# The first FFN's pools of a one-core encoder layer end ahead of its low-rank stage

## The chip, the cores and the metric

The kernel runs on one core of a Trainium2 chip. The core has a matrix engine (TensorE, PE in the profile), three engines for elementwise work (VectorE or DVE, ScalarE or ACT, GpSimd or POOL), SyncE (SP), which issues most transfers, and 16 DMA engines. Tiles lie in on-chip memory with 128 rows (partitions); matrix products land in PSUM, eight banks of 128 × 512 words. What counts is the device time of one launch in microseconds (us).

## The reference, cut to what matters

The kernel computes one layer for 1024 tokens of width 1024, in float32:

```python
x = x + 0.5 * post1(FFN1(pre1(x)))             # SwiGLU, hidden width 2816
z = pre2(x) @ w_in                             # attention q|k|v, then r|k|v, decay-, iclr-, gate-down
# attention group: 8 heads, rotary, three dilated bands
# RWKV-7 group: u = u + mu_prev * (prev - u) + mu_next * (next - u), then
w_logit = w0 + jnp.einsum('bsdr,drc->bsdc', jnp.tanh(wd), w2)      # wd: 2 directions x 64
decay = jnp.exp(-jnp.exp(-jax.nn.softplus(-w_logit) - 0.5))
a = jax.nn.sigmoid(a0 + jnp.einsum('bsdr,drc->bsdc', ad, a2))      # ad: 2 directions x 64
# ... forward and backward delta-rule scans with decay, a, k, v, r; gate with g
x = x + post2(concat(attn, rwkv) @ w_out)
x = x + 0.5 * post3(FFN2(pre3(x)))
```

The two lines with `w2` and `a2` are the low-rank stage: from 64 numbers per token and direction to 512, for the decay and for the in-context rate.

## The kernel before, in words

The layer runs as a chain of stages. FFN1 and FFN2 form their products in blocks with fewer multiplications than the plain product needs. Every large product is done in a split form: both factors are cut into a high and a low part (names that end in h and l), and three products, high × high, low × high, high × low, are added up in PSUM. ACT makes the high part, DVE the low one.

FFN1 ends in `down`, which hands finished token tiles to `hand_over`; this adds the residual, stores h1 and turns the normalised tiles into the operand x2. Half of the tokens at a time, `ready` (in `run`) then projects three column tiles of w_in, 12, 13 and 14: the inputs of decay, rate and gate. Their products are still named gu, with weights gh and gl. `finish_low` brings them out of PSUM (ACT: us and u), forms the token shift on DVE, and for decay and gate a tanh. `low_rank` is called for "w" (decay) and "a" (rate). For each of two directions it builds weights w (tile name rh) and the low part `low` (rl), and two operands rx, each with 64 rows of high parts and 64 of low parts. For four groups of 128 channels and two halves of the tokens it makes two products into one bank (lg): rh by rx over 128 rows, and rl by rx over the 64 rows of the high part:

```python
T.matmul(q, w[:, cs], x[half], start=True, stop=False)
T.matmul(q, low[hs, cs], x[half][hs], start=False, stop=True)
```

That makes 64 lg products. ACT takes a tanh from each pair into ra; for the decay ACT then scales ra, DVE forms a running sum in it (a scan, reset at every chunk by the tile `reset`), and SP stores ra to DRAM as d_w or d_a. The scan stage later loads these back as th_w and th_a.

Next come `project_rwkv` (products zr, 576 of them) and `project_tokens` (zq, 1152), with weights loaded as zraw by SP and split into zh (ACT) and zl (DVE). Then attention is interleaved with the preparation (`prep`: lp and others), solution and chaining of the scan's chunks, followed by the gate and normalisation, `out_project` (products pw), and FFN2.

Nothing of this runs in the order in which it is written. A recorder, `_Tape`, notes all operations; `wire` finds which must follow which, also through the reuse of tiles and banks; `cost` gives each a duration; `sweep` lists them by rank, and the table LEADS adds an amount to the ranks of stretches of recorded operations (from, to, lead). `GATED` names groups of products that are to start only when their inputs are due. `play` (line 486) then issues everything, each engine in its fixed order. So every instruction has the line of `play`, and is told by its tile's names.

Two kinds of pool matter. A pool's memory is handed to later pools when it closes; `ffn1` and `hand1` (tiles gh, gl, junk) and the PSUM pool `ps_1` (tags gu and d, four banks each) close at the end of the `with` block, after `low_rank`; the pool `zr`, opened behind it, lies over the place of the FFN1 pools. The `ring` is the weight ring that lives through the whole kernel (tags raw, wh, wl, tmp).

## Time and profile before

| | us |
|---|---|
| median of 3 runs | 2276.98 (2271.82 to 2277.48) |
| profiled execution | 2268.24 |
| its span in the profile | 2266.4 |
| TensorE busy | 2177.2 (96%) |
| last gu of FFN1's end, start | 712.87 |
| lg products, first and last start | 713.10, 750.8 |
| first zr, start | 754.90 |
| first lp, start | 876.3 |

The profile shows one execution. A row of a timeline has the start, the duration, the engine, the operation with its output and inputs, and in brackets how long the engine stood idle before it and what it then waited for. PE's durations overlap, since products are pipelined; how long a product occupies PE is read from one start to the next. A row of windows gives, for a stretch, the busy time and number of instructions of each engine, then the clock that was granted to TensorE (1.00 is full speed), the busy share of the DMA engines and their rate.

### The profile page before, as it was taken

The page shows a single profiled execution, that of the slowest core. Times are in us where ns is not written, and L with a number is a line of the kernel's source. Part 1 is how long each engine was busy: PE and PEld are TensorE (multiplying, and loading weights), DVE is VectorE, ACT ScalarE, POOL GpSimd, SP SyncE. Part 2 cuts the span into 40 slices and gives each one's busy share as a digit, 9 for nine tenths or more (in the row PEclk, how much of TensorE's full clock was granted, in tenths as well). Part 3 has the DMA queues.
Part 4 walks back from the last instruction along what each step waited for, and adds up shares of the span by engine and source line. Part 5 has one row for each costly group of instructions (what it writes and reads, how often), then busy time and mean ns, then how long its engine had stood idle before and what let it go on. Part 6 is the DMA issues. An engine that isn't in the chain of part 4 may idle for free. (4 is left out here: it accounts for less than half of the span.)

```text
span 2266.4 us, 41176 instructions
## 1 busy us (share of the span) xinstructions
PE 2177.2 (96%) x15236; PEld 1793.6 (79%) x15236; DVE 1499.2 (66%) x2606; ACT 1059.0 (47%) x2031; POOL 708.2 (31%) x1034
## 2 busy tenths in 40 slices
PE   7999999999999999999789998998899999999998
PEld 5888888888876688999768787776688888888886
DVE  8767767775586345772464658647987777777566
ACT  6333333354578445452556666455533333325453
POOL 2244444520000000557275562131024444452000
PEclk9999999999998899999798999999999999999999
DMA  5354444586662537773896675597535544458665
GB/s 148 117 166 166 160 158 148 194 291 193 189 209 81 208 110 199 196 227 111 239 223 166 157 182 136 144 299 261 158 103 175 169 158 158 140 200 296 193 201 183
DMA packets 373054, 408.71 MB, mean 180 GB/s; under 512 B 76659, under 2 KB 279283, under 8 KB 372853
## 3 DMA queue, kind: packets, MB, share of 16 engines
q1 hardware_dynamic: 324096, 303.18, 45.0%
q0 software_dynamic: 30704, 94.44, 11.9%
q10 hardware_dynamic: 18052, 8.46, 1.4%
q8 instruction: 120, 1.97, 0.4%
q14 instruction: 82, 0.66, 0.1%
HBM read 271.69 MB, written 134.28 MB: 179 GB/s over the span
## 5 line engine op out<-in xcount | busy, mean ns | idle before, releaser
L486 ACT ACTIVATE wh<-raw 128x512 fp32r<-128x512 f32 x264 | 162.8, 628 | 378.9 <-PE gu L486 313.4
L486 DVE TENSOR_TENSOR row<-gu,row 128x512 f32<-128x512 f32 x308 | 204.3, 686 | 108.0 <-PE gu L486 64.2
L486 DVE TENSOR_TENSOR wl<-raw,wh 128x512 fp32r<-128x512 f32 x264 | 215.2, 824 | 88.2 <-ACT wh L486 55.8
L486 POOL TENSOR_TENSOR row<-row 128x512 f32<-128x512 f32 x88 | 123.7, 1406 | 435.3 <-DVE row L486 424.2
L486 PE MATMUL gu<-xh,wh 128*128 128x512 f32 x704 | 250.1, 394 | 0.6 <-DVE row L486 0.6
L486 PE MATMUL gu<-xl,wh 128*128 128x512 f32 x704 | 249.0, 392 | 0.2 <-DVE xl L486 0.2
L486 PE MATMUL gu<-xh,wl 128*128 128x512 f32 x704 | 248.9, 391 | 0.0
L486 DVE TENSOR_TENSOR gwl<-graw,gwh 128x512 fp32r<-128x512 f32 (+1 forms) x176 | 112.0, 642 | 111.7 <-PE pd L486 80.4
L486 PE MATMUL pd<-gh,gwl 128*128 128x512 f32 x616 | 181.3, 391 | 0.5 <-DVE gwl L486 0.5
L486 PE MATMUL pd<-gh,gwh 128*128 128x512 f32 x616 | 180.7, 391 | 0.0
L486 PE MATMUL pd<-gl,gwh 128*128 128x512 f32 x616 | 180.5, 390 | 0.0
L486 ACT ACTIVATE gwh<-graw 128x512 fp32r<-128x512 f32 (+1 forms) x176 | 100.6, 576 | 140.9 <-PE pd L486 115.8
L486 PEld LDWEIGHTS gu<-xh,wh 128*128 128x128 f32 x704 | 133.2, 190 | 28.1 <-DVE row L486 1.0
L486 PEld LDWEIGHTS gu<-xl,wh 128*128 128x128 f32 x704 | 132.6, 189 | 27.6 <-DVE xl L486 0.5
L486 PEld LDWEIGHTS gu<-xh,wl 128*128 128x128 f32 x704 | 132.2, 188 | 27.4 <-issue 0.2
L486 PEld LDWEIGHTS pd<-gh,gwl 128*128 128x128 f32 x616 | 115.7, 188 | 25.4 <-DVE gwl L486 1.1
L486 PEld LDWEIGHTS pd<-gh,gwh 128*128 128x128 f32 x616 | 115.6, 188 | 24.1
L486 PEld LDWEIGHTS pd<-gl,gwh 128*128 128x128 f32 x616 | 115.7, 188 | 23.9
L486 ACT ACTIVATE gh<-raw 128x512 fp32r<-128x512 f32 x160 | 99.2, 629 | 51.9 <-PE pd L486 31.0
L486 POOL TENSOR_TENSOR ws<-ws 128x512 f32<-128x512 f32 x88 | 119.9, 1362 | 3.0
L486 DVE TENSOR_TENSOR gl<-raw,gh 128x512 fp32r<-128x512 f32 x160 | 114.4, 722 | 9.0 <-ACT gh L486 8.9
L486 POOL DMA_DIRECT2D d_hid<-row x154 | 83.7, 547 | 90.3 <-DVE row L486 76.0
(299 smaller groups left out, 5130.6 us busy)
## 6 DMA issues: line engine op xcount, KB each, us to landing
d_hid<-row POOLq DMA_DIRECT2D x154, 256.0 KB, 2.7
graw<-d_hid SPq DMA_DIRECT2D x132, 256.0 KB, 2.7
raw<-in_ffn_w_gate_dram SPq DMA_DIRECT2D x88, 256.0 KB, 3.2
raw<-in_ffn_w_up_dram SPq DMA_DIRECT2D x88, 256.0 KB, 3.1
ws<-in_ffn_w_down_dram SPq DMA_DIRECT2D x88, 256.0 KB, 3.7
d_ws<-ws POOLq DMA_DIRECT2D x88, 256.0 KB, 2.9
raw<-d_ws SPq DMA_DIRECT2D x88, 256.0 KB, 3.5
raw<-in_ffn_w_down_dram SPq DMA_DIRECT2D x66, 256.0 KB, 3.7
```

The costliest lines, as they stand in the source:

```text
L486: i = getattr(getattr(self.nc, op.eng), op.method)(*op.args, **op.kwargs).ins
```

## The change

The pools ffn1, hand1 and ps_1 get a stack of their own, s_f1, which closes after `finish_low` and ahead of `low_rank`. `low_rank` takes its tiles rh, rl and rx from the ring's tags wh and wl, and its banks from a new pool ps_l of three. `reset` becomes a 512-wide tile in the ring, and the pools for the next stages (pw, po, zr) open ahead of `low_rank`. The second half's gu products of `ready` use the banks with tag d. The unused half of the rl rows is zeroed by GpSimd, and the second lg product runs over all 128 rows. The scaling of the decay goes from ACT to DVE, in halves of 512, and so does the scan. The three mixing constants are loaded at the start of the kernel. The products of `out_project` are renamed op and enter GATED. The scheduler's costs change for transfers with 64 rows or fewer, for long 64-row products and for DVE's tensor_scalar. LEADS is another table, with 45 entries in place of 27, so that instructions move all over the kernel.

```diff
@@ -35,12 +35,16 @@
 LEADS = (
-    (173, 348, -479), (1428, 1481, 2437), (1440, 1452, 10001), (2180, 2899, 3481), (8375, 8561, 532),
...
+    (173, 304, -13864), (735, 754, -5727), (1432, 1454, -4125), (1676, 1677, -11252), (2515, 2520, -13828),
@@ -98,7 +102,7 @@
     FREE, NEAR = ("ps_w",), 3000
-    GATED = {"s3": 0, "s12": 0, "pt3": 0, "pt12": 0, "lp": 0, "bp": 0, "yq": 0, "gate": 1, "bonus": 1}
+    GATED = {"s3": 0, "s12": 0, "pt3": 0, "pt12": 0, "lp": 0, "bp": 0, "yq": 0, "gate": 1, "bonus": 1, "op": 2}
 
@@ -220,7 +224,7 @@
                         for op in users.get(name, ()):
-                            if op.eng != "tensor":
+                            if op.eng != "tensor" or self.GATED[base] == 2:
                                 given[first].update((g, 1) for g in given[op] if g.eng is None or self.GATED[base] and g.eng != "tensor")
@@ -260,9 +264,10 @@
         if op.method == "dma_start":
-            op.took, op.late = (560 if op.eng == "gpsimd" else 360), 1500
             runs = [math.prod(q[1] for q in a.ap) // (a.ap[-1][1] if a.ap[-1][0] == 1 else 1) for a in (x, *op.ins)]
             size = math.prod(q[1] for q in x.ap) * 4
+            half = any(a.tensor.name in self.home and a.ap[0][1] <= 64 for a in (x, *op.ins))
+            op.took, op.late = (560 if op.eng == "gpsimd" else 360) + 200 * half, 1500 + (600 if half else 0)
             op.moved = (14 * max(runs) + 0.0384 * size) / 16
@@ -272,7 +277,7 @@
             elif w.dtype == F32R:
-                op.took = max(58, 13 + 0.418 * n)
+                op.took = max(58, 13 + 0.418 * n) * (2 if n > 256 and k <= 64 else 1)
             elif m <= 32:
@@ -282,7 +287,7 @@
             rate = 1.04
-            if op.method in ("tensor_copy", "memset") and all(
+            if op.method in ("tensor_copy", "tensor_scalar", "memset") and all(
                     self.home.get(a.tensor.name, (None,))[0].space != PSUM for a in op.ins if a.tensor.name in self.home):
@@ -764,9 +769,9 @@
 
-    def product(self, psum, x, hl, which):
-
-        return self.product_into([psum.tile([128, 512], F32, name="gu", tag="gu") for _ in which], x,
+    def product(self, psum, x, hl, which, tag="gu"):
+
+        return self.product_into([psum.tile([128, 512], F32, name="gu", tag=tag) for _ in which], x,
                                  [(h[:, k, :], l[:, k, :]) for h, l in hl for k in range(4)], which)
@@ -989,20 +994,21 @@
 
-    def low_rank(self, p, ring, rows, psum, nm, y, reset):
+    def low_rank(self, ring, rows, psum, nm, y, reset):
 
...
         raw = self.slab(ring, self.io["rwkv_" + nm + "2"].rearrange("o d r (a b) -> (o d r) a b", a=4)).rearrange("p a b -> p (a b)")
-        low = p.tile([128, 512], F32R, name="rl", tag="gh", bufs=GB)
         bias = self.w0h if nm == "w" else self.a0h
+        tile = lambda name, tag: ring.tile([128, 512], F32R, name=name, tag=tag, bufs=WB)
         for d in range(2):
             hs, os = slice(d * 64, d * 64 + 64), slice(64 - d * 64, 128 - d * 64)
-            w = p.tile([128, 512], F32R, name="rh", tag="gh", bufs=GB)
+            w, low = tile("rh", "wh"), tile("rl", "wl")
             A.activation(w[hs], raw[hs], AF.Copy)
             A.activation(w[os], raw[hs], AF.Copy)
+            self.nc.gpsimd.memset(low[os].bitcast(F32), 0.0)
             V.tensor_tensor(low[hs], raw[hs], w[hs], op=OP.subtract)
-            x = [p.tile([128, 512], F32R, name="rx", tag="gl", bufs=GB) for half in range(2)]
+            x = [tile("rx", t) for t in ("wh", "wl")]
             for half in range(2):
@@ -1013,12 +1019,14 @@
                     T.matmul(q, w[:, cs], x[half], start=True, stop=False)
-                    T.matmul(q, low[hs, cs], x[half][hs], start=False, stop=True)
+                    T.matmul(q, low[:, cs], x[half], start=False, stop=True)
                     sl = slice(half * 512, half * 512 + 512)
...
                 if nm == "w":
-                    A.activation(o, o, AF.Copy, scale=-0.5 * DECAY, bias=-0.5 * DECAY)
-                    V.tensor_tensor_scan(o, reset, o, 0.0, op0=OP.mult, op1=OP.add)
+                    for half in range(2):
+                        c = o[:, half * 512:half * 512 + 512]
+                        V.tensor_scalar(c, c, -0.5 * DECAY, -0.5 * DECAY, op0=OP.mult, op1=OP.add)
+                        V.tensor_tensor_scan(c, reset, c, 0.0, op0=OP.mult, op1=OP.add)
                 self.nc.sync.dma_start(self.lr_d[nm][d][pr], o)
@@ -1548,7 +1556,7 @@
             for dh in range(2):
-                ps = psum.tile([128, 512], F32, name="pw", tag="w")
+                ps = psum.tile([128, 512], F32, name="op", tag="w")
                 self.out_products(ps, W, dh, xh, xl, ts)
@@ -1584,6 +1592,7 @@
     def mix_columns(self):
+        self.mix_constants(self.cons)
         nc, io, G, p = self.nc, self.io, self.nc.gpsimd, self.cons
@@ -1672,16 +1681,17 @@
                 s_pg.close()
-                psum = self.pool(st, "ps_1", 4, space=PSUM)
+                s_f1, s_pl = ExitStack(), ExitStack()
+                psum = self.pool(s_f1, "ps_1", 4, space=PSUM)
                 x2, low, ps = [], {}, {}
-                p = self.pool(st, "ffn1")
-                hand = self.pool(st, "hand1")
+                p = self.pool(s_f1, "ffn1")
+                hand = self.pool(s_f1, "hand1")
                 gb = self.row_bcast(hand, "ffn1_post_g")
...
                     for ct in LO:
-                        ps[ct, half] = self.product(psum, x2, low[ct], (half,))[0]
+                        ps[ct, half] = self.product(psum, x2, low[ct], (half,), ("gu", "d")[half])[0]
 
@@ -1693,19 +1703,21 @@
                 x = x2
-                reset = hand.tile([128, S], F32, name="reset", tag="junk")
+                y = [self.finish_low(rows, psum, ct, [ps[ct, half] for half in range(2)]) for ct in LO]
+                s_f1.close()
+                s_at, s_sc, s_ps, s_zr, s_sp, s_bl = (ExitStack() for _ in range(6))
+                NB, blk, s_ba, s_bb, s_pw, s_mt = NC_ // BLK, {}, ExitStack(), ExitStack(), ExitStack(), ExitStack()
+                pw = self.pool(s_pw, "ps_w", 4, space=PSUM, **R)
+                po = _Banks(w=pw, o=self.pool(s_ps, "ps_o", 1, space=PSUM))
+                pl = self.pool(s_pl, "ps_l", 3, space=PSUM)
+                zr = self.pool(s_zr, "zr", 2)
+                reset = ring.tile([128, 512], F32, name="reset", tag="tmp", bufs=TMP)
                 nc.gpsimd.memset(reset, 1.0)
                 nc.gpsimd.memset(reset[:, 0::C], 0.0)
-                y = [self.finish_low(rows, psum, ct, [ps[ct, half] for half in range(2)]) for ct in LO]
-                self.low_rank(p, ring, rows, psum, "w", y[0], reset)
-                self.low_rank(p, ring, rows, psum, "a", y[1], reset)
-            s_mc, s_at, s_sc, s_ps, s_zr, s_sp, s_bl = (ExitStack() for _ in range(7))
-            self.mix_constants(self.pool(s_mc, "mixc", **R))
-            NB, blk, s_ba, s_bb, s_pw, s_mt = NC_ // BLK, {}, ExitStack(), ExitStack(), ExitStack(), ExitStack()
-            pw = self.pool(s_pw, "ps_w", 4, space=PSUM, **R)
-            po = _Banks(w=pw, o=self.pool(s_ps, "ps_o", 1, space=PSUM))
+                self.low_rank(ring, rows, pl, "w", y[0], reset)
+                self.low_rank(ring, rows, pl, "a", y[1], reset)
+                s_pl.close()
             pc = self.pool(s_ps, "ps_c", 1, space=PSUM)
-            zr = self.pool(s_zr, "zr", 2)
             self.project_rwkv(zr, po, x, [(4, 2), (6, 2), (0, 2), (2, 2), (8, 2), (10, 2)])
@@ -1828,7 +1840,6 @@
             s_xn.close()
-            s_mc.close()
 
...
```

On PE at the end of FFN1 (gu is the projection of the three low-rank column tiles, lg the low-rank products, zr the next projection), the kernel before has

```order
L486 MATMUL gu<-xl_1336,gh 128x512
L486 MATMUL gu<-xh_1335,gl 128x512
L486 MATMUL lg<-rx,rh 128x512 x4
L486 MATMUL lg<-rx,rl 128x512 x4
L486 MATMUL lg<-rx,rh 128x512
L486 MATMUL lg<-rx,rl 128x512
```

with zr only behind all 64 lg. The changed kernel has there

```order
L491 MATMUL gu<-xl_1339,gh 128x512
L491 MATMUL gu<-xh_1338,gl 128x512
L491 MATMUL zr<-xh_1336,zh 128x512
L491 MATMUL zr<-xh_1338,zh 128x512
L491 MATMUL zr<-xl_1337,zh 128x512
L491 MATMUL zr<-xh_1336,zl 128x512
```

and its first lg behind 296 zr products:

```order
L491 MATMUL zr<-xh_1336,zl 128x512
L491 MATMUL zr<-xh_1338,zl 128x512
L491 MATMUL lg<-rx,rh 128x512 x2
L491 MATMUL zr<-xl_1337,zh 128x512
L491 MATMUL zr<-xl_1339,zh 128x512
L491 MATMUL zr<-xh_1336,zh 128x512
L491 MATMUL zr<-xh_1338,zh 128x512
L491 MATMUL lg<-rx,rl 128x512 x2
L491 MATMUL zr<-xh_1336,zl 128x512
L491 MATMUL zr<-xh_1338,zl 128x512
```

The lg moved from ahead of zr into zr; 116 zr products stand between the first of the 64 and the last.

On SP at the same place (d_w and d_a are the stores of low-rank results, th_w and th_a their loads for the scan, zraw the weights of zr), before:

```order
L486 DMA d_a_112<-ra 128x1024 x2
L486 DMA d_w_109<-ra 128x1024
L486 DMA d_a_112<-ra 128x1024
L486 DMA th_w<-d_w_109 128x4x128
L486 DMA d_a_112<-ra 128x1024
L486 DMA d_a_115<-ra 128x1024 x2
L486 DMA th_a<-d_a_112 128x4x128
L486 DMA d_a_115<-ra 128x1024
L486 DMA zraw<-in_w_in_dram 128x256 x4
```

and with the change:

```order
L491 DMA zraw<-in_w_in_dram 128x256 x4
L491 DMA rope<-in_k_rope_dram 128x128 x2
L491 DMA zraw<-in_w_in_dram 128x256 x36
L491 DMA d_w_106<-ra 128x1024 x4
L491 DMA zraw<-in_w_in_dram 128x256 x2
L491 DMA d_w_109<-ra 128x1024 x2
L491 DMA d_a_112<-ra 128x1024
L491 DMA d_w_109<-ra 128x1024
L491 DMA d_a_112<-ra 128x1024
L491 DMA zraw<-in_w_in_dram 128x256 x2
```

The first 40 loads of zraw moved from behind the stores to a place ahead of them; later ones stand between them.

On ACT at the same place (us and u are evacuations of gu, ra the tanh of lg, zh the split of zraw), before:

```order
L486 ACTIVATE ra<-lg,w0h 128x512 x4
L486 ACTIVATE ra<-ra 128x1024 x2
L486 ACTIVATE ra<-lg,a0h 128x512 x7
L486 ACTIVATE e_2412<-th_w 128x8x64
L486 ACTIVATE ra<-lg,a0h 128x512 x7
L486 ACTIVATE th_w<-th_w 128x512
L486 ACTIVATE ra<-lg,a0h 128x512 x2
L486 ACTIVATE zh<-zraw 128x256 x12
```

and with the change:

```order
L491 ACTIVATE us<-gu,mu_289 128x512 x3
L491 ACTIVATE u<-gu 128x512 x3
L491 ACTIVATE us<-gu,mu_289 128x512 x2
L491 ACTIVATE u<-gu 128x512 x2
L491 ACTIVATE zh<-zraw 128x256 x4
L491 ACT_TABLE_LOAD
L491 ACTIVATE us<-us 128x1024
L491 ACTIVATE zh<-zraw 128x256 x4
```

The first split of zr's weights moved from behind all tanhs to directly behind the evacuations of gu.

At FFN2's entry 16 of the transposes (pt) that feed it stand ahead of the last 48 op products, where before 28 followed the last pw.

14 rows, old and new, of the table LEADS are left out of this document.

## The prediction

> **What bounds the kernel now.** I read three views: the page's totals and chain of waits, then the stages as windows, then the timeline of PE (TensorE) where the stages show a hole.
>
> ```profile
> PE 2177.2 (96%) x15236; PEld 1793.6 (79%) x15236; DVE 1499.2 (66%) x2606; ACT 1059.0 (47%) x2031; POOL 708.2 (31%) x1034
> PE gu L486 18%; PE pd L486 9%; PE po L486 1%; DVE row L486 1%; PE pw L486 1%; DMA wor<-in_w_out_dram 1%; DMA f_y<-d_y 0%; DVE Ti L486 0%; DVE ttmp L486 0%; PE pt L486 0%; DMA in<-d_rk 0%; PE yc L486 0%; DVE raw L486 0%; DVE wl L486 0%; DVE xl L486 0%
> ```
>
> PE is busy 96% of the span and heads the chain, so only what PE does or waits for counts. But busy is not the same as fast. The windows (length; then busy us and instruction count of PE, PEld, DVE, ACT, POOL; then granted clock, DMA share, GB/s) show where PE is busy at a low clock:
>
> ```profile
> 0.00:55.00 55.00, 40.41 (x168) 29.85 (x169) 46.63 (x78) 34.84 (x64) 12.64 (x24) 0.97 0.52 149
> 660.00:712.00 52.00, 51.47 (x245) 41.88 (x244) 32.79 (x51) 38.97 (x68) 2.65 (x9) 1.00 0.38 114
> 712.00:752.00 40.00, 36.95 (x70) 16.20 (x68) 25.90 (x17) 33.62 (x52) 0.55 (x1) 0.58 0.56 220
> 752.00:910.00 158.00, 154.81 (x867) 126.86 (x868) 71.20 (x119) 72.93 (x145) 10.12 (x17) 0.98 0.51 155
> 910.00:1070.00 160.00, 158.82 (x1682) 153.89 (x1681) 98.73 (x259) 71.08 (x187) 98.21 (x164) 1.00 0.63 183
> 1070.00:1400.00 330.00, 300.37 (x4816) 252.80 (x4814) 183.47 (x474) 202.78 (x462) 169.29 (x359) 0.92 0.73 183
> 1600.00:1660.00 60.00, 50.93 (x264) 42.16 (x264) 56.63 (x89) 33.86 (x62) 1.50 (x2) 0.91 0.41 134
> ```
>
> The third row is the stage that the change takes apart: 70 matmuls in 40 us at clock 0.58, between stages at 1.00 and 0.98. On either side PE is full (51.47 of 52, 154.81 of 158), so time saved between them moves all that follows. PE's timeline (start, us, operation, [idle before, releaser]) tells how it is lost:
>
> ```profile
> 712.87 0.39 PE L486 MATMUL gu<-xh,gl 128*128 128x512 f32 x1
> 713.10 1.07 PE L486 MATMUL lg<-rx,rh 128*128 128x512 f32 x4
> ...
> 716.22 0.50 PE L486 MATMUL lg<-rx,rh 128*128 128x512 f32 x1
> 716.65 0.50 PE L486 MATMUL lg<-rx,rl 64*128 64x512 f32 x1
> ...
> 720.52 0.80 PE L486 MATMUL lg<-rx,rh 128*128 128x512 f32 x1 [1.18 <-ACT ra L486]
> ...
> 727.03 0.79 PE L486 MATMUL lg<-rx,rh 128*128 128x512 f32 x1 [1.24 <-ACT ra L486]
> 727.75 0.79 PE L486 MATMUL lg<-rx,rl 64*128 64x512 f32 x1
> 728.47 1.22 PE L486 MATMUL lg<-rx,rh 128*128 128x512 f32 x2
> ...
> 750.23 1.22 PE L486 MATMUL lg<-rx,rl 64*128 64x512 f32 x2
> 754.90 1.22 PE L486 MATMUL zr<-xh,zh 128*128 128x512 f32 x2 [3.45 <-ACT zh L486]
> ...
> 758.48 0.90 PE L486 MATMUL zr<-xl,zh 128*128 128x512 f32 x2
> 759.22 0.62 PE L486 MATMUL zr<-xh,zl 128*128 128x512 f32 x2
> 759.68 0.63 PE L486 MATMUL zr<-xh,zh 128*128 128x512 f32 x2
> 760.15 0.62 PE L486 MATMUL zr<-xl,zh 128*128 128x512 f32 x2
> ```
>
> A long product costs PE the distance to the next start. At full clock that is 712.87 to 713.10, 0.23 (0.227 over longer runs: 759.22 to 759.68 is 0.46 for two). Where the 128-row product rh and the 64-row product rl alternate it is 0.43 (716.22 to 716.65) while the clock is still high, and 0.72 (727.03 to 727.75) once it has fallen. ACT causes two short waits, 2.4 us in all; the rest of the 41.8 us from 713.10 to 754.90 is alternation, half clock and a 3.45 us gap before zr, the next projection. That gap has its own cause:
>
> ```profile
> 750.05 0.32 SPq L486 DMA_DIRECT2D d_a<-ra  x1
> 750.41 2.45 SPq L486 DMA_DIRECT2D zraw<-in_w_in_dram  x4
> ...
> 754.43 1.50 ACT L486 ACTIVATE zh<-zraw 128x256 fp32r<-128x256 f32 x4 [2.11 <-DMA zraw<-in_w_in_dram]
> ```
>
> The first weights of zr are asked for at 750.41, behind the stores d_w and d_a of low-rank results on SP's queue, and ACT can only then split them.
>
> **The change, part by part.** *Low rank leaves the path.* After the change PE goes from the last gu straight to zr: 296 zr products stand ahead of the first lg, and the 64 lg lie among the next 116. They stay PE work, but are 128-row products among 128-row products, so 64 × 0.227 = 14.5 us is their cost. Removed: 41.8 − 14.5 = 27.3. The first ten zr after the hole took 754.90 to 759.22, 4.3 us against 2.3 at full clock: 2.0 more. Together 29.3 us are there to be won.
>
> *A new hand-over.* The first zr needs zh, which on ACT stands behind the evacuations (us, u) of the last two gu tiles. Their zraw loads now stand ahead of the low-rank stores on SP and wait only for products of FFN1, long past.
>
> ```profile
> 711.05 1.27 ACT L486 ACTIVATE us<-gu,mu 128x512 f32<-128x512 f32 x2
> 712.21 1.08 ACT L486 ACTIVATE u<-gu 128x512 f32<-128x512 f32 x2
> 713.30 0.69 ACT L486 ACTIVATE us<-gu,mu 128x512 f32<-128x512 f32 x1
> ```
>
> Four evacuations at 0.56 (711.05 to 713.30 is four) and one zh at 0.4 (four in 1.50) are 2.7 us. Bounds: 0.4, were the evacuations done, and the 3.45 of before. I take 2.7, since both last tiles end together at the end. After this gap the clock may fall: 0 to 2.0 us as after 754.90. I take 1.0, since the row of before had been at half clock ahead of its gap and so cannot tell which.
> By the Trainium skill, TensorE: Matmul & The Clock Gate, section on the HAM clock gate, the clock drops after an idle window of about 3.4 us; a gap of 2.7 us would then keep full speed, this 1.0 would be 0 and the sum 1 us better. Against it stands this trace's fall from 0.43 to 0.72 a product, which comes with waits of only 1.2 us.
>
> *ACT and the lg banks.* Each pair of lg holds one of three banks until ACT's tanh has read it.
>
> ```profile
> L486 ACT ACTIVATE ra<-lg,a0h x16: 677/687/688, 734.8 to 751.6; 128x512 f32<-128x512 f32 x16
> L486 ACT ACTIVATE ra<-ra x8: 1038/1060/1068, 717.9 to 733.9; 128x1024 f32<-128x1024 f32 x8
> L486 DVE TENSOR_TENSOR_SCAN ra<-reset,ra x8: 2262/2266/2292, 719.0 to 737.1; 128x1024 f32<-128x1024 f32 x8
> L486 SPq DMA_DIRECT2D d_w<-ra x8: 319/320/613, 721.4 to 739.4; - x8
> ```
>
> Most pairs have enough zr between them to cover 0.69 us; the last dozen stand with one zr between, a pair each 3 × 0.227 = 0.68, about ACT's own pace while ACT also evacuates zr. Bounds: 0, and 1.2 (the waits above) for each of 32 pairs, 38. I take 2.0, near the 2.4 of before.
>
> *Work that changes engine.* The decay scaling leaves ACT (8 × 1.06 = 8.5 us less) for DVE: sixteen halves, never seen here in that form, between 0.35 and 0.7 each (half of an ACT pass would be 0.53): 6 to 11 us. The scans stay 8 × 2.27 = 18.1 whether halved or not. In the stage that now holds them DVE has 71 of 158 us and comes to some 100, ACT has 73 and comes to 73 + 32 × 0.69 = 95: both covered. Uncovered, DVE's share alone would cost its 11. The zeroing of the padded rows is four tiles on POOL, which has 10 of 158: nothing.
>
> *The head.* Three small constant loads move into it, on SP, at 0.32 to 0.6 each: up to 1.8 us. The new order makes DVE split the first weights sooner and PE's first products stand earlier among its transposes. The waits view (total us, times, longest) and one row of the timeline bound what that can bring:
>
> ```profile
> PE pt L486 <- DVE xl L486: 15.3, 9, 5.4
> ...
> PE pt L486 <- DVE row L486: 3.4, 2, 1.9
> ...
> 1615.54 2.79 PE L486 MATMUL pt<-ident,row 128*128 128x128 f32 x12 [5.43 <-DVE xl L486]
> ```
>
> Of 15.3 us of transposes waiting for DVE, 5.4 is at FFN2's entry and 9.9 in the head. DVE is busy 46.6 of the head's 55 us, so most of it stays: I take −1.5, from −4 to +2.
>
> *FFN2's entry.* Sixteen transposes now stand ahead of the last out-projection products, instead of 28 after them. The waits there are 5.43 + 3.4 = 8.8 us, but DVE is busy 56.6 of 60. I take −2.0, from −8.8 to 0.
>
> *Attention and scan.* The same products in another order. PE waits 29.6 of 330 us between 1070 and 1400; I can give no sign to a new order there: 0, from −8 to +8, about a quarter of these waits.
>
> **Sum.** −29.3 + 2.7 + 1.0 + 2.0 − 1.5 − 2.0 = −27.1. The profiled execution took 2268.24 us (span 2266.4 and 1.84 around it) and should become 2241. It lies 8.7 below the median of the three runs, 2276.98; taking the saving from the median gives 2250.
>
> **Rivals.** (1) *The low-rank results come late, and some gain is given back.* They are used by lp, the first product of the scan (the landing rows are of the stores d_w and d_a, then of the loads th_w):
>
> ```profile
> L486 PE MATMUL lp<-pr,bk x512: 271/272/580, 876.3 to 1434.7; 64*128 64x128 f32 x171
> ...
> DMA to landing us min/median/max: 2.6/3.7/4.9
> ...
> L486 ACT ACTIVATE e<-th_w x16: 614/629/635, 742.0 to 1418.9; 128x512 f32<-128x512 f32 x16
> ...
> DMA to landing us min/median/max: 4.4/6.1/8.8
> ```
>
> With zr from 715.8 (713.1 + 2.7), the last lg would end 412 + 64 products later, 824, and lp's turn come after 503 + 64 products, 844; both 2 later with the waits. Between them lie tanh 0.7, scaling and scan 1.8, store 3.7, load 6.1 and about 2 for e and two products: 14 of 20 us. So 6 us of slack, with SP's queue mixing these loads with zraw loads that wait for buffers. If they come 20 us late, 14 are lost: 2264. For it: the small slack; against it: the first direction's stores stand ahead in the queue.
>
> (2) *The entries give more.* Head −4 and FFN2 −8.8 in place of −3.5 together: 2241. For it, the waits exist; against it, DVE's 56.6 of 60.
>
> (3) *PE stalls at every lg, and the kernel is slower.* In the old order PE had nothing else; now a zr stands behind each lg, and ACT serves us, u and zh between the tanhs. At 1.24 us for each of 32 pairs it is 39.7 instead of 2.0: 2288. It decides from (27.1 + 2.0) / 32 = 0.91 us a pair. Against it: ACT's load, and two waits among 32 pairs in the denser order of before.
>
> (4) *The clock falls among the lg.* If short waits lower the clock, the 180 products from the first lg to the last cost up to 180 × (0.43 − 0.227) = 37 us more; over half of them 18: 2268. The trace has such a fall at waits of 1.2 us, but there the 64-row products alternated too.
> The Trainium skill names this in the same page, section on a second HAM failure mode: short idles from cycling PSUM banks make the clock swing. The stage from 910 to 1070, which cycles banks too, does not agree: its clock is 1.00.
>
> That low rank still stands alone is ruled out by the order of instructions.
>
> **How the numbers follow.** Forecast 0.60, rival (1) 0.16, (2) 0.12, (3) 0.06, (4) 0.06. A difference under 0.3% (6.8 us) is about what a measurement of this kernel cannot tell from none. Half of (4) and 0.02 of the forecast, where attention loses 20 us, fall within it: same 0.05. Rival (3) is slower 0.06, the rest faster 0.89. The forecast's own bounds are 2236 (gap 0.4, no half clock, no waits, attention −8) to 2266 (gap 3.45, half clock 2.0, waits 5, twice those of before, entries 0, attention +8). The range reaches past (1): 2232 to 2267, leaving out (3), half of (4) and the outer tails.
>
> **What would show it.** Right: zr within 3 us of the last gu, the stage's clock back above 0.95, no lg in a 64-row shape, lp's first start near 846. Wrong: lg waits of over 10 us on ACT; lp waiting for DVE bk or th_w (1); a clock of 0.8 or less between 780 and 830 (4); more than 38 us of PE waits in the stretch that was 1070 to 1400 and now begins some 25 earlier.

## The result

The changed kernel takes 2259.7 us (median of 9 runs, 2253.7 to 2272.18) against 2273.62 for the kernel before (9 runs beside it, 2267.39 to 2288.01): a ratio of 0.9939, interval 0.9913 to 0.9965, so 0.6% faster, some 14 us. Forecast were 27 us, from 2277 to 2250; the time lies inside the range, with half of the saving.

The hole between FFN1 and zr is gone. PE's timeline after the change, at the place where before the lg began:

```profile
710.30 0.39 PE L491 MATMUL gu<-xh,gl 128*128 128x512 f32 x1
712.74 0.72 PE L491 MATMUL zr<-xh,zh 128*128 128x512 f32 x2 [2.06 <-ACT zh L491]
...
714.74 0.63 PE L491 MATMUL zr<-xh,zh 128*128 128x512 f32 x2
715.21 0.62 PE L491 MATMUL zr<-xl,zh 128*128 128x512 f32 x2
...
828.33 0.39 PE L491 MATMUL lg<-rx,rh 128*128 128x512 f32 x1
828.55 0.39 PE L491 MATMUL lg<-rx,rl 128*128 128x512 f32 x1
828.78 0.39 PE L491 MATMUL zr<-xh,zh 128*128 128x512 f32 x1
829.00 0.39 PE L491 MATMUL lg<-rx,rh 128*128 128x512 f32 x1
```

The first zr follows the last gu by 2.4 us instead of standing at 754.90, 2 us on, two zr take 0.47 (full clock), and far behind, the lg lie among zr at 0.227 each with no wait. ACT shows what the gap is: two evacuations each of us and u, then zh.

```profile
710.04 1.37 ACT L491 ACTIVATE us<-gu,mu 128x512 f32<-128x512 f32 x2 [0.33 <-PE gu L491]
711.31 1.07 ACT L491 ACTIVATE u<-gu 128x512 f32<-128x512 f32 x2
712.26 1.34 ACT L491 ACTIVATE zh<-zraw 128x256 fp32r<-128x256 f32 x4
```

The windows of the changed kernel: over the place of the old hole, around the lg, from the first zr to the last zq (1063.5), and from there to the last out-projection product (1610.8):

```profile
712.00:755.00 43.00, 41.71 (x242) 33.64 (x243) 29.55 (x48) 29.31 (x54) 2.68 (x5) 1.00 0.36 123
790.00:832.00 42.00, 42.00 (x187) 34.77 (x186) 34.88 (x48) 30.59 (x53) 3.27 (x9) 1.00 0.58 226
...
712.70:1063.50 350.80, 345.70 (x2720) 309.12 (x2720) 207.07 (x425) 173.58 (x381) 121.14 (x211) 0.99 0.60 183
1063.50:1610.80 547.30, 489.28 (x6555) 390.23 (x6554) 325.17 (x745) 304.52 (x655) 205.19 (x379) 0.89 0.71 189
```

and the same late stretch of the kernel before, whose last zq starts at 1089.9 and whose last pw at 1603.7:

```profile
1089.90:1603.70 513.80, 471.07 (x6547) 377.69 (x6546) 316.23 (x739) 302.52 (x651) 196.76 (x372) 0.93 0.73 200
```

So the change leads by 26.4 us at the last zq, and is 7.1 late at the last out-projection product: the stretch between took 547.3 instead of 513.8 us for the same work. PE was busy 18.2 longer in it, at a lower clock (0.89 against 0.93), and idle 15.3 longer (58.0 against 42.7). This profiled execution, 2272.18 us, was the slowest of the nine; that of before, 2268.24, one of the quick ones. What of this comes from the change and what from the execution was the first thing to find out.

One statement on the kernel before needs mending: the ring is not one for the whole kernel. FFN1's ring closes with its block, behind `low_rank`, and FFN2 has its own.

### The profile page after: what moved, and what is told of

Read it like the earlier page. It is cut to its first block, busy times and chain, and to the rows that moved or that the text cites. A ratio compares the mean times of both kernels' runs of the same rounds, so it can differ in the third digit from the quotient of the medians.

```text
span 2270.4 us, 41200 instructions
## 1 busy us (share of the span) xinstructions
PE 2175.3 (96%) x15236; PEld 1799.2 (79%) x15236; DVE 1519.2 (67%) x2630; ACT 1051.3 (46%) x2023; POOL 720.1 (32%) x1038
## 4 chain that ended last, share of the span: by engine, by line
PE 81%; DMA 6%; DVE 5%; POOL 2%; issue 2%; ACT 2%; SPq 1%; DVEq 0%; ACTq 0%; POOLq 0%
PE gu L491 37%; PE pd L491 17%; PE zr L491 5%; PE zq L491 5%; PE po L491 3%; PE pt L491 2%; PE lp L491 2%; DVE row L491 2%; PE s L491 2%; PE xu L491 2%; POOL Ti L491 1%; PE y L491 1%; POOL ttmp L491 1%; SPq L491 1%; DMA X<-d_x 1%
## 5 line engine op out<-in xcount | busy, mean ns | idle before, releaser
L491 POOL TENSOR_TENSOR row<-row 128x512 f32<-128x512 f32 x88 | 129.3, 1469 | 447.6 <-DVE row L491 420.2
L491 ACT ACTIVATE gwh<-graw 128x512 fp32r<-128x512 f32 (+1 forms) x176 | 101.0, 577 | 137.0 <-PE pd L491 113.2
L491 POOL DMA_DIRECT2D d_hid<-row x154 | 83.8, 547 | 81.6 <-DVE row L491 67.6
```

The lines of the kernel that those rows point to most:

```text
L491: i = getattr(getattr(self.nc, op.eng), op.method)(*op.args, **op.kwargs).ins
```

## The experiments

**The same kernel again.**

```diff
 # the changed kernel, unaltered
```

> The changed kernel once more, for a second profile. Theory A: the start is as in the first profile (first zr 712.7, last zq 1063.5, 26 us ahead of the kernel before) whatever the execution, and what an execution loses against that it loses between 1064 and 1620, in attention, scan and out-projection; the last op product, 7 us later than the last pw of before in the first profile, comes 8 to 15 us ahead of it (1589 to 1596) in an execution of median length. Rival B, the late stages are as they are in every execution: the last op again within 3 us of 1610.8. Time 2254 to 2266.

Measured: 2256.03 us against 2270.4 (0.9938, 0.9916 to 0.996). Last zq 1061.6, 28.3 ahead of the kernel before; last op 1598.7, 5.0 ahead, outside the 8 to 15 of theory A and far from rival B's 1610.8.

```profile
1061.60:1598.70 537.10, 479.56 (x6555) 382.86 (x6554) 323.38 (x745) 304.70 (x655) 204.80 (x379) 0.91 0.71 193
```

The start repeats within 2 us. The late stretch does not: 537.1 against 547.3, and the difference is all busy time (479.6 against 489.3 for the same instructions, clock 0.91 against 0.89); PE is idle 57.5 and 58.0. So of the two losses one is steady, some 15 us more waiting than before, and one is the clock, whose cost differs by 10 us between these two executions.

**The 64-row products back, order unchanged.**

```diff
-                    T.matmul(q, low[:, cs], x[half], start=False, stop=True)
+                    T.matmul(q, low[hs, cs], x[half][hs], start=False, stop=True)
```

(the planner counts them as 128 rows, so that every engine's order stays as it is)

> The second lg product over 64 rows again, the order of all instructions unchanged; the zeroed rows stay but are not read. Theory A: where shapes alternate each change costs 0.2 us at full clock (0.43 against 0.227 in the kernel before); rl stands in 21 groups among full-row products, so 42 changes, 8.4 us more up to the last zq (1072 instead of 1063.5), the clock between 780 and 830 stays above 0.9, and the time is 5 to 9 us longer. Rival C, it was the 64-row shape that brought the clock down: clock 0.5 to 0.7 between 780 and 830 and 25 us or more lost. Rival D, among many full-row products the shape costs nothing and the whole saving came from moving the stage: within 2 us of the changed kernel at the last zq.

Measured: 2269.15 us (0.9997, 0.9979 to 1.0015 to the kernel before). Last zq at 1069.6: 8.0 later than in the second profile of the change (1061.6), where 8.4 was worked out. PE among the lg:

```profile
822.54 0.40 PE L491 MATMUL lg<-rx,rh 128*128 128x512 f32 x1
822.87 0.50 PE L491 MATMUL lg<-rx,rl 64*128 64x512 f32 x1
823.30 0.50 PE L491 MATMUL zr<-xl,zh 128*128 128x512 f32 x1
823.64 0.40 PE L491 MATMUL lg<-rx,rh 128*128 128x512 f32 x1
```

and the window around them (the clock is the third number from the end):

```profile
790.00:832.00 42.00, 42.00 (x163) 28.51 (x162) 34.55 (x46) 25.38 (x44) 2.32 (x5) 1.00 0.48 183
```

Three products take 1.10 from 822.54 to 823.64, where three full-row ones take 0.68: 0.42 for a change of shape and back, at clock 1.00. Rivals C (the shape brings the clock down here) and D (it costs nothing) fall. From the first lg to the last it takes 48.8 us, against 40.6 in both profiles of the change. The delay of 8 us at the last zq is still there at the last op (1606.9, 8.2 later) and at the end (span 2266.9 against 2258.6). That suggests that what arrives late leaves late, but it is one pair of profiles, and two executions of the change alone differ by 12 us. By the medians of the same round the loss is 13 us (2269.15 against 2256.03), above the 5 to 9 expected; what makes up the difference is open.

**Padding alone, in the kernel before.**

```diff
             w = p.tile([128, 512], F32R, name="rh", tag="gh", bufs=GB)
+            low = p.tile([128, 512], F32R, name="rl", tag="gh", bufs=GB)
+            self.nc.gpsimd.memset(low[os].bitcast(F32), 0.0)
...
-                    T.matmul(q, low[hs, cs], x[half][hs], start=False, stop=True)
+                    T.matmul(q, low[:, cs], x[half], start=False, stop=True)
```

> The kernel before with the second lg product over 128 rows alone, the added rows zeroed by GpSimd, and every engine's order as before. Theory A: alone on the path the stage is bound by ACT and DVE in its first 20 us (both busy 9.8 of 10 there) and by PE after, so the clock rises but first zr moves only from 754.9 to 744 to 751, and the time falls by 4 to 10 us. Rival C, the shape was all: lg at 0.227 each, first zr at 735 or earlier, time 18 us or more shorter. Rival E, ACT and the stores ahead of zraw bound it throughout: first zr within 2 us of 754.9, no gain.

Measured: 2271.69 us (1.001, 0.9995 to 1.0025): no gain, rival E. The windows of that stage:

```profile
722.00:732.00 10.00, 6.38 (x17) 3.95 (x16) 9.91 (x8) 9.95 (x16) 0.00 (x0) 0.78 0.45 185
732.00:742.00 10.00, 8.30 (x26) 5.24 (x25) 7.12 (x4) 9.78 (x17) 0.00 (x0) 0.83 0.84 329
742.00:755.00 13.00, 1.74 (x6) 1.14 (x6) 0.77 (x3) 4.02 (x9) 0.00 (x0) 0.69 0.93 339
```

and the timeline at its end, of SP's queue, ACT and PE:

```profile
748.04 0.37 SPq L753 DMA_DIRECT2D th_a<-d_a  x1
748.46 0.60 SPq L753 DMA_DIRECT2D d_a<-ra  x1
749.10 2.58 SPq L753 DMA_DIRECT2D zraw<-in_w_in_dram  x4
...
753.78 1.40 ACT L753 ACTIVATE zh<-zraw 128x256 fp32r<-128x256 f32 x4 [8.98 <-DMA zraw<-in_w_in_dram]
...
754.25 1.22 PE L753 MATMUL zr<-xh,zh 128*128 128x512 f32 x2 [11.26 <-ACT zh L753]
```

The products got faster (PE busy 6.4 of 10 where it had been 8.8) and the last lg starts 8.2 us earlier; PE then waits 11.26 for zh instead of 3.45. ACT is full for 20 us; in the last 13 it is not (4.02), and the zraw loads still go out only at 749, behind the stores d_a and a load of what they store (th_a). So PE's speed did not hold the hole open. What ends it is that queue; the DMA engines are also 0.93 busy there, and how much is SP's order and how much their load was not told apart. The padding saved its 8 us only where the lg stand among other products.

**The late stages by the old ranks.**

```diff
+        # from the first operation behind the projections on: rank as in the kernel before
+        for op, rank in zip(self.ops[7893:], RANKS_OF_BEFORE):
+            op.rank = rank
         return self.sweep()[0]
```

> All operations recorded behind the projections (scan preparation, attention, scan, finish, out-projection, FFN2) get the ranks that the kernel before gave them, so that their order is near that of before; up to the projections the order is that of the change. Theory A, the new order gives gain back in attention: the last zq stays at 1064 and the lead of 26 us over the kernel before holds to the last out-projection product (1580 to 1586 instead of 1610.8); time 2246 to 2252. Rival B, the late stages give it back in any order, since they wait for transfers and for the solution of the chunks: time 2256 to 2264, as the changed kernel.

Measured: 2289.79 us (1.0088, 1.0063 to 1.0113). The last zq comes at 1060.3 but the last op at 1629.0. Neither theory had this. It tells little, since the planner made a third order of these ranks; the exact late order of before, below, puts the question properly.

**More buffers for the out-projection's weights, order unchanged.**

```diff
-                raw = p.tile([128, 512], F32, name="wor", tag="wor", bufs=2)
+                tag = "wor" if gain is not None else ("yat", "wor", "wor", "yah", "yal")[(2 * k + dh) % 5]
+                raw = p.tile([128, 512], F32, name="wor", tag=tag, ...)
```

> The changed kernel, every engine's order as it is, but the raw tiles of the second half of w_out (wor) lie in five buffers in turn, the two of before and three whose attention tiles (yat, yah, yal) are dead by then. In the second profile of the change the last attended product (po) starts at 1501.7, yet wor is loaded two by two from 1506.8 to 1528.1 and the first op product starts at 1532.0. Theory F, the two buffers are what lets the lead shrink there from 21 us to 5: wor's last load by 1515, first op 1518 to 1526, last op 1585 to 1593 instead of 1598.7, time 2246 to 2252 against 2256. Rival G, the finish units (yc, which wait for f_y out of the scan) set it: first op within 3 us of 1532, time 2253 to 2260.

Measured: 2261.51 us (0.9946, 0.9923 to 0.997); first op 1534.7, last 1599.8. No gain, as rival G had it, and the time just above its 2253 to 2260. The loads did not come sooner either (last wor at 1531.0), since on SP each stands behind transfers for the finish units:

```profile
1508.32 2.32 SPq L760 DMA_DIRECT2D wor<-in_w_out_dram  x2
1511.96 2.37 SPq L760 DMA_DIRECT2D f_k<-d_kd  x2
1514.38 0.93 SPq L760 DMA_DIRECT2D wor<-in_w_out_dram  x2
1516.92 0.38 SPq L760 DMA_DIRECT2D f_k<-d_kd  x1
```

So with SP's order as it is, the buffers are not the limit; whether they would be in another order was not tried. That the finish units are, is what is left and was not shown by itself here.

**The gate on op.**

```diff
-    GATED = {..., "op": 2}
+    GATED = {..., "op": 1}
```

> The op products gated as gate and bonus are (1) in place of 2, so that in the planned order the first product of a tile need not stand behind all of its weights; without any gate the planner finds no order. The planner lays out all engines anew from this. Theory H, the gate delays op: first op by 1524, last op by 1594, time 2248 to 2254. Rival, the gate is harmless and the buffers or finish units decide: last op within 4 us of 1598.7, time 2254 to 2264.

Measured: 2286.77 us (1.0081, 1.0053 to 1.011). First op 1529.4, last 1614.6, but attention too comes later (its last product by 13 us against the second profile), for the planner laid out everything anew. Theory H gets no support; what the gate does by itself stays open.

**Both kernels without their tables.**

```diff
-LEADS = ( ... )
+LEADS = ()
```

> The changed kernel without its table LEADS; to be compared with the next, the kernel before without its table. Theory A, the structure alone (pools closed early, padded products, low rank among zr) gives the 26 us of the front and keeps at least half: this one 13 to 26 us shorter than the next. Rival I, the gain needs the new table: within 6 us of each other, or the lg again ahead of zr.

> The kernel before without its table LEADS. Low rank still alone between the last gu and the first zr, a hole of 40 to 46 us; the time 10 to 60 us above the kernel before, since the order of attention was set with the table.

Measured: 2286.56 us (1.0071, 1.005 to 1.0092) and 2290.67 (1.0093, 1.0071 to 1.0115 to the kernel before; 18.5 us above it, inside the 10 to 60). The structure alone brings 38 us at the first zr, but 15.9 at the last zq, where theory A had 26, and 4.1 in the end: rival I in the time. The late stretch again takes longer in the changed structure:

```profile
1072.40:1621.80 549.40, 479.90 (x6554) 389.58 (x6553) 327.34 (x746) 300.64 (x653) 201.62 (x379) 0.89 0.69 188
```

against, without the table, in the structure of before

```profile
1088.30:1621.10 532.80, 469.97 (x6547) 377.12 (x6546) 317.70 (x740) 302.60 (x650) 197.98 (x373) 0.93 0.71 193
```

9.9 us more busy (0.89 against 0.93) and 6.7 more idle. So the loss is not a flaw of one table.

**The late order of before, exactly.**

```diff
+        # every engine's queue: up to the last zr as the change has it,
+        # from the first zq on as the kernel before has it
+        time = {op: KEYS[op.n] for op in self.ops}
+        queue = {e: sorted((op for op in self.ops if op.eng == e), key=time.get) for e in self.NAMES}
```

> The changed kernel up to the last zr in its own order; from the first zq on, every engine takes its instructions in exactly the order of the kernel before (op ungated, under the name op). The second profile of the change leads by 28 us at the last zq and by 5 at the last out-projection product, and 8 us of delay put in at the front by the 64-row products came out whole at the end, so nothing independent of the front ends these stages. Theory A, the new order of the late stages loses the rest: here the lead stays above 20 us to the last op (1576 to 1584), time 2244 to 2251. Rival B, the late stages lose it in either order (transfers and the scan's own chain, met at another moment): last op 1592 to 1602, time 2254 to 2264.

Measured: 2263.78 us (0.9955, 0.9939 to 0.9972); last zq 1081.4, last op 1598.8. Last op and time are rival B's, but not its path: the lead shrinks from 27.9 us behind the last lg to 8.8 at the end of the first quarter of zq, and from there it is nearly kept, 8.5 at the last zq and 4.9 at the last op.

```profile
1081.40:1598.80 517.40, 476.08 (x6547) 382.19 (x6546) 319.42 (x739) 302.74 (x651) 196.79 (x372) 0.93 0.73 199
```

The stretch is 517.4 with PE idle 41.3: the old order brings the old waits back. PE's timeline behind the splice and the waits of the whole span (total us, times, longest):

```profile
845.12 0.63 PE L775 MATMUL vt<-ident,us 128*128 128x128 f32 x4 [2.79 <-DVE us L775]
```

```profile
PE xu L775 <- DMA sv<-d_vt: 4.6, 1, 4.6
```

With the old order PE waits where it did not in the new one (vt 2.8, xu 4.6). Both rows are of the tiles of v, transposed (vt) and loaded back (sv), not of low-rank results: that the old order loses the lead because these come late, as the next expectation has it, is not shown. From the first zr to the last zq PE is idle 16.3 us here, against 4.2 in the second profile of the change, and busy 7 us longer at a lower clock. That the new order keeps 28 us up to the last zq is thus work of the order too.

**Spliced behind the last zq.**

```diff
+        # as the change up to the last zq; what its plan has later, as the kernel before
```

> The changed kernel in its own order to the last zq; every instruction that its plan has later than that stands in the order of the kernel before. With the whole late order of before the lead fell from 28 to 9 us between the last zr and the first quarter of zq, and from there on stayed within 4 us to the end (8.6 to 4.9). Theory A: the order of the change is right up to the last zq, since it puts the late low-rank results where they come, and the order of before is right from there: lead 24 to 28 us at the last zq and 20 to 26 at the last op product (1578 to 1584), time 2246 to 2253, 8 to 14 us under the changed kernel. Rival B, the stages behind zq lose the lead in any order when it is this large: last op 1592 or later, time 2255 to 2264.

Measured: 2255.12 us (0.9935, 0.9914 to 0.9956), the lowest median here, though not to be told from the changed kernel's 0.9938 and 0.9939. Last zq 1060.2, 29.7 ahead; last op 1588.9, 14.8 ahead, between the two theories.

```profile
1060.20:1588.90 528.70, 481.57 (x6547) 386.91 (x6546) 319.24 (x739) 303.36 (x651) 201.13 (x378) 0.91 0.72 195
```

PE idles 47.1, ten less than in the new order and four more than before. Busy is 481.6, as in the second profile of the new order and 10.5 over before, at a clock of 0.91. So in the profile the old order saves the waits, and the clock's part stays. The time hardly shows it: the last op comes 9.8 us sooner than in the second profile of the change, but FFN2's entry gives 2.8 back, that profile was the slowest of its four executions, and the medians, 2255.12 and 2256.03, differ by 0.9. What takes up the rest is open.

**Spliced behind attention.**

```diff
+        # as the change to the end of attention; what its plan has later, as the kernel before
```

> As the other, spliced later: the order of the change to the end of attention, that of before for the last scan chunks, the finish units, out-projection and FFN2. Theory A: in the second profile of the change the lead is 21 us at the last attended product and 5 at the last op; here it stays 15 to 21 to the last op (1583 to 1589), time 2250 to 2257. Rival B: last op 1595 or later, time 2256 to 2264.

Measured: 2272.58 us (1.0006, 0.9991 to 1.0021). Last op 1610.4, as rival B said, with a time above its range, but by a cause that neither had: a wait of the scan for a transfer, 18.7 us at 1426, where the change waits 4.7 at most. It holds up the last attended product (1528.0, 26 us later than in the second profile of the change).

```profile
PE pa L773 <- DMA d<-d_t: 29.3, 5, 18.7
```

Behind that wait the old order does what theory A had of it: from the last attended product to the last op it takes 82.4 us, where the change took 95.0 and 96.5 and the kernel before 80.4.

**The kernel before again.**

```diff
 # the kernel before, unaltered
```

> The kernel before once more, for a second profile of it. Counted in the stretch from the last zq to the last out-projection product, TensorE stood at clock 0.5 for 68 us in the first profile (of 514 us), 75 in both variants with the same late order behind a start of nearly the same time, but 96 and 116 in the two profiles of the change (537 and 547 us) and 92 in the spliced order (529 us). Theory J, the late stages lose the lead mostly by more half clock: here again 60 to 80 us, and a stretch of 478 to 484 us plus half of it. Rival, the half clock there is chance from one execution to the next: 90 us or more in one of two executions of the same kernel, and then the stretch 10 us or more longer than 514.

Measured: 2272.53 us (one run).

```profile
1090.30:1608.10 517.80, 473.93 (x6546) 380.84 (x6546) 316.37 (x739) 303.19 (x651) 198.66 (x372) 0.92 0.73 199
```

78.5 us at half clock by the trace's own clock records, and 517.8 us long: inside theory J's 478 to 484 plus half of 78.5, and the rival, chance, did not show. That the half clock is most of the loss does not follow: idle time grew by 14 to 15 us, busy time by 6 to 18. All profiles of this stretch beside each other (us; idle is length less busy, half clock is from the clock records, the next column counts it from the first zq on, and the end is from the last attended product, po, to the last op):

| kernel | last zq | length | idle | half clock | from first zq | end |
|---|---|---|---|---|---|---|
| before, twice | 1089.9, 1090.3 | 513.8, 517.8 | 42.7, 43.9 | 68, 78.5 | 75, 85 | 80.4, 80.0 |
| before, padded | 1088.6 | 519.4 | 45.6 | 75 | 82 | 81.6 |
| before, no table | 1088.3 | 532.8 | 62.8 | 75 | 78.5 | 94.4 |
| late order of before | 1081.4 | 517.4 | 41.3 | 75 | 89 | 80.2 |
| spliced behind zq | 1060.2 | 528.7 | 47.1 | 92 | 92 | 80.8 |
| spliced behind attention | 1062.4 | 548.0 | 69.7 | 99 | 99 | 82.4 |
| change, twice | 1063.5, 1061.6 | 547.3, 537.1 | 58.0, 57.5 | 116, 96 | 123, 96 | 95.0, 96.5 |
| change, 64 rows | 1069.6 | 537.3 | 55.9 | 102 | 102 | 94.9 |
| change, five buffers | 1060.6 | 539.2 | 55.5 | 109 | 109 | 93.5 |
| change, no table | 1072.4 | 549.4 | 69.5 | 116 | 126 | 100.2 |
| change, gate 1 | 1065.1 | 549.6 | 60.4 | 130 | 133 | 92.1 |
| change, old ranks | 1060.3 | 568.6 | 72.1 | 137 | 137 | 101.0 |

Idle goes by the order: 41 to 47 in the old, 55 to 58 in the new, more in the other orders. The end does too: 80 to 82 us in the six profiles that have the order of before there, 93 to 97 in the four with the order of the change. Half clock is below 80 wherever the stretch begins behind 1080, and above 90 wherever it begins before 1073. Part of that is only where the count begins: with the same order behind the last zq, 75 and 92 become 89 and 92 when counted from the first zq. So it is not shown that an earlier start brings more half clock. Idle time alone does not bring it either: before without its table idles 63 and has no more of it. Nor does the chip: the padded kernel (75) and the second profile of the change (96) ran on one chip, the second profile of before (78.5) and the first splice (92) on another. What brings it stays open; no run kept the clock up there.

## Why the prediction was half right

**What held.** *The hole.* That alternating shapes, half clock and a queue made it, and that zr at once would win it back, is what the profiles show. Lead at the last zq: 26.4 and 28.3, where removal (−29.3), gap, half clock, lg waits (+5.7) and head (−1.5) came to 25.1. *The gap* was 2.06 us idle, 2.7 forecast, by the very instructions named. *The half clock behind it* was none in the first profile and 3.4 us in the second, which costs 1.7 at most, 1.0 forecast. *The waits of lg* were none, 2.0 forecast, so rival (3) falls. *The head* gave 1.6 and 1.4 at the first pd, 1.5 forecast. *FFN2's entry*: from the last out-projection product to the end of the span 659.6 and 659.9 us against 662.7 (and 662.7 again in the splice, which has the old order there): 2.8 to 3.1, 2.0 forecast. *DVE's new work* was covered, the scaling near its lower bound, the scans above what was taken for them:

```profile
L491 DVE TENSOR_SCALAR ra<-ra x16: 402/421/430, 793.6 to 822.9; 128x512 f32<-128x512 f32 x16
L491 DVE TENSOR_TENSOR_SCAN ra<-reset,ra x16: 1197/1218/1225, 794.0 to 826.9; 128x512 f32<-128x512 f32 x16
```

The scaling is 16 × 0.42 = 6.7 us, 6 to 11 forecast. The scans are 16 × 1.22 = 19.5, not the 8 × 2.27 = 18.1 "whether halved or not".

**What failed** is the term "attention and scan: 0, from −8 to +8". It measured 33.5 and 23.3 us in the two profiles, and about 16 by the medians (27 + 3 − 14). That the time still lies in the range is luck: the range reached up to 2267 for rival (1), not for this. The step behind the term was that the same products in another order have no sign. The loss had two parts. The new order waits 15 us more, in both executions alike; the waits view of the second profile names transfers and finish units that before hardly appear (pa 1.3, yc 2.4, bonus 0 for these in the first profile of before):

```profile
PE pa L491 <- DMA d<-d_t: 11.6, 3, 4.1
PE yc L491 <- POOL f_y L491: 8.9, 4, 5.6
PE bonus L491 <- DVE f_k L491: 3.2, 2, 3.0
```

All of the yc and bonus waits lie at the end, from the last attended product to the last op. The windows of that piece, for the kernel before, the second profile of the change and the order spliced behind the last zq:

```profile
1523.30:1603.70 80.40, 74.21 (x492) 53.35 (x491) 61.40 (x94) 43.97 (x91) 11.28 (x9) 0.98 0.74 238
1502.10:1598.70 96.60, 80.03 (x482) 57.46 (x482) 68.76 (x108) 48.76 (x100) 18.71 (x14) 0.91 0.69 226
1508.00:1588.90 80.90, 72.80 (x492) 52.31 (x491) 62.26 (x94) 44.04 (x91) 11.14 (x9) 1.00 0.74 237
```

It is 16 us longer in the change, ten of them idle (16.6 against 6.2), and back to its length in the old order. The sign that the prediction named for a loss in attention, more than 38 us of PE waits in a stretch of 330 us, did not show: from 1045 to 1375 they are 29.3 and 27.2 us in the two profiles. The waits came behind it.

The other part is that TensorE stands more at half clock, which costs 6 to 18 us of busy time. A bound of a quarter of the waits of before was too narrow: it took the idle time of one stage as what can change, and left out the stages behind it and the clock, though the row of that stage (0.92) said that it was below full speed.

**Rival (1)** had the loss and the size (14 us given back), not the place: lp started 22 us earlier than before (at 853.4 and 854.9, later than the 846 forecast) and waited 1.1 us in all for bk. Beyond that no row shown here has PE held up by a late low-rank result. **Rival (4)** named the clock but among the lg, where it stayed at 1.00; it fell in the stages behind. The stage from 910 to 1070, which the prediction set against short idles as a cause, is no test of it: PE idles only 1.2 of its 160 us. **Rival (2)** came true in FFN2's 3 us, no more.

*On the rule weighed there:* the Trainium skill, TensorE: Matmul & The Clock Gate, section on the HAM clock gate, has the clock fall after an idle window of about 3.4 us. By it a gap of about 2 us keeps full speed. The first profile agrees, at 1.00 from 712 to 755; the second has 0.96 there for the same gap. Of the eight profiles here with this gap of 2.06 us, four have the clock at half for 3.4 us close behind it, so the rule is no safe bound here. The fall that the prediction set against the rule is misread there: the clock records put it at 718.12, ahead of the first of the two waits, which begins at 719.3. It did not come with the waits.

## What to carry to other kernels

A stage that PE crosses at half speed can be worth its whole length only if what follows takes the time over: set the lead at each boundary beside the forecast, down to the last short stage, and expect an order of thousands of instructions, made for another start, to need making again. Pad short products when they stand among full ones; here it bought nothing where they stood alone ahead of a late load. And read a stage's PE time as waits and clock apart: busy time is no constant of the instructions.

## What the runs showed of the hardware that was not expected

Two executions of one program, at the same order, spent 479.6 and 489.3 us of busy time on the same 6555 products, at a clock of 0.91 and 0.89 (96 and 116 us at half); that is most of the 12 us by which they differed. A change between a 64-row and a 128-row product and back cost 0.42 us at full clock, in a stream without a wait. The low clock of the old hole came with hardly any idle time, as the kernel before shows:

```profile
717.94 0.67 PE L486 MATMUL lg<-rx,rh 128*128 128x512 f32 x1
718.54 0.79 PE L486 MATMUL lg<-rx,rl 64*128 64x512 f32 x1
...
722.00:732.00 10.00, 8.76 (x15) 3.69 (x14) 9.90 (x8) 9.95 (x16) 0.00 (x0) 0.50 0.44 180
732.00:742.00 10.00, 10.00 (x17) 4.46 (x17) 7.39 (x4) 7.28 (x12) 0.00 (x0) 0.50 0.81 316
```

The clock fell at 718.12, after 679 us at full speed, four us behind the first 64-row product (714.10) and ahead of PE's first wait. From 722 to 742 PE is busy 18.8 of 20 us, at 0.50; padded to full rows, with more idle time (busy 14.7 of 20), it was 0.78 and 0.83. Between 712 and 755 the three profiles with 64 rows alone on the path have 36.6 to 36.9 us at half clock, the padded one 18.4. Where the 64-row products stood among zr, one product in three or fewer, the clock stayed at 1.00. So the close alternation of shapes had a part in the low clock, beside the waits; how the clock weighs them is not shown.
